# Issuing the first load ahead of the entry barrier in a row-wise relu-and-mean kernel

## The chip, the cores and the metric

The kernel runs on one core of a Trainium2 chip. The metric is device time in microseconds (us) per execution, taken as the median over several executions. "Span" is the length of one profiled execution, from its first to its last profiled instruction. The measured time of the same execution is 1.78 us longer than the span, in the kernel before (164.37 against 162.59).

Engine names in the profile: DVE is VectorE, ACT is ScalarE, POOL is GpSimd, SP is SyncE. A `q` behind a name (SPq) is the engine's sequencer: issues, semaphores, drains.

## The reference

```python
def setup_inputs():
    batch, seq, dim = 32, 512, 1024
    return {"x": np.random.randn(batch, seq, dim).astype(np.float32)}

def reference(x):
    relu_x = np.maximum(x, 0)
    return np.mean(relu_x, axis=-1).astype(np.float32)
```

The input is 64 MiB, the output 64 KiB. Each input value is used once.

## The kernel before

The input is seen as 128 partitions of 128 rows of 1,024 values. Seven loads bring 16 rows per partition each (8 MiB); the last 16 rows come in shrinking pieces, so that little work is left when the last byte lands. ACT and DVE take the rows in turn, each with one call that applies the relu and sums the row (in the profile, one long instruction and a short read of the sum).

```python
    in_pool = ctx.enter_context(tc.tile_pool(name="in", bufs=3))
    ...
    def rows(xt, lo, n, j0):
        for k in range(lo, lo + n):
            j = j0 + k
            (dve_row if j % 2 else act_row)(nc, xt[:, k, :], sums[:, j:j + 1])
    ...
    for t in range(full):                    # full = 7
        j0 = t * NB                          # NB = 16
        xt = in_pool.tile([P, NB, D], F32, name="xt")
        nc.sync.dma_start(out=xt, in_=xr[:, j0:j0 + NB, :])
        rows(xt, 0, NB, j0)
    ...
    for n in row_pieces:                     # 8, 4, 2, 1 rows
        nc.sync.dma_start(out=xt[:, lo:lo + n, :], in_=xr[:, j0 + lo:j0 + lo + n, :])
        lo += n
    for w in col_pieces:                     # the last row: 512, 256, 256 columns
        nc.sync.dma_start(out=last[:, c:c + w], in_=xlast[:, c:c + w])
        c += w
    ...                                      # the last rows, then the store of the result
```

With three buffers, the first three loads wait for nothing; each later one waits until its buffer has been read.

Ahead of all this stands an entry block that the kernel's author doesn't write. POOL sets four constants there, and then all five engines meet: PE, ACT, DVE and SP each run a drain, which adds one to a gather semaphore, and wait; POOL runs its own drain, waits for a count of four, and releases them. In the kernel before, SyncE's first load comes behind that wait.

Of the kernel before, what the change touches and what calls it, by code (L numbers as in the profile page):

```python
# [1 line left out]

# [4 lines left out]

F32 = mybir.dt.float32
ALU = mybir.AluOpType
ACT = mybir.ActivationFunctionType  # L10


def act_row(nc, src, acc):

    nc.scalar.activation(out=src, in_=src, func=ACT.Relu, accum_out=acc)  # L15


def dve_row(nc, src, acc, init=None):

    nc.vector.tensor_scalar(  # L20
        out=src, in0=src, scalar1=0.0, scalar2=init,
        op0=ALU.max, op1=ALU.add, accum_out=acc,
    )


@with_exitstack
def kernel(
    ctx: ExitStack,
    tc: tile.TileContext,
    x: bass.AP,  # L30
    out: bass.AP,
):
    nc = tc.nc
    P = nc.NUM_PARTITIONS
    xf = x.flatten_outer_dims()
    R, D = xf.shape
    assert R % P == 0
    J = R // P
    inv = 1.0 / D
    xr = xf.rearrange("(p j) d -> p j d", p=P, j=J)  # L40
    outr = out.flatten().rearrange("(p j) -> p j", p=P, j=J)
    xlast = xr[:, J - 1, :]

    NB = 16
    full = J // NB - 1

    row_pieces = [8, 4, 2, 1]
    assert sum(row_pieces) == NB - 1
    col_pieces = [512, 256, 256]
    assert sum(col_pieces) == D  # L50

    in_pool = ctx.enter_context(tc.tile_pool(name="in", bufs=3))
    res_pool = ctx.enter_context(tc.tile_pool(name="res", bufs=1))
    sums = res_pool.tile([P, J], F32)
    res = res_pool.tile([P, J], F32)
    part = res_pool.tile([P, 10], F32)
# [7 lines that stand above are left out]
    def finish(lo, hi):  # L64
        nc.gpsimd.tensor_scalar(  # L65
            out=res[:, lo:hi], in0=sums[:, lo:hi], scalar1=inv, scalar2=0.0, op0=ALU.mult, op1=ALU.add,
        )

    for t in range(full):
        j0 = t * NB  # L70
# [4 lines that stand above are left out]
    j0 = full * NB  # L75
    xt = in_pool.tile([P, NB, D], F32, name="xt")
    prev, last = xt[:, NB - 2, :], xt[:, NB - 1, :]
    lo = 0
    for n in row_pieces:
        nc.sync.dma_start(out=xt[:, lo:lo + n, :], in_=xr[:, j0 + lo:j0 + lo + n, :])  # L80
        lo += n
    c = 0
    for w in col_pieces:
        nc.sync.dma_start(out=last[:, c:c + w], in_=xlast[:, c:c + w])
        c += w

    finish(0, j0)
    lo = 0
    for n in row_pieces[:-1]:
        rows(xt, lo, n, j0)  # L90
        lo += n
    finish(j0, j0 + lo)



    act_row(nc, prev[:, :512], part[:, 0:1])
    dve_row(nc, prev[:, 512:], part[:, 1:2])
    nc.gpsimd.tensor_scalar(  # L98
        out=res[:, J - 2:J - 1], in0=part[:, 0:1], scalar1=part[:, 1:2], scalar2=inv, op0=ALU.add, op1=ALU.mult,
    )  # L100
    act_row(nc, last[:, :256], part[:, 2:3])
    dve_row(nc, last[:, 256:512], part[:, 3:4])
    nc.gpsimd.tensor_scalar(  # L103
        out=part[:, 4:5], in0=part[:, 2:3], scalar1=inv, scalar2=0.0, op0=ALU.mult, op1=ALU.add,
    )
    act_row(nc, last[:, 512:640], part[:, 5:6])
    dve_row(nc, last[:, 640:768], part[:, 6:7], init=part[:, 3:4])
    nc.scalar.activation(  # L108
        out=part[:, 7:8], in_=part[:, 5:6], func=ACT.Identity, scale=inv, bias=part[:, 4:5],
    )  # L110
    dve_row(nc, last[:, 768:], part[:, 8:9], init=part[:, 6:7])
    nc.vector.scalar_tensor_tensor(  # L112
        out=res[:, J - 1:J], in0=part[:, 8:9], scalar=inv, in1=part[:, 7:8], op0=ALU.mult, op1=ALU.add,
    )
    nc.sync.dma_start(out=outr, in_=res)


# [1 line left out]
_INS = ['x']  # L119
_OUTS = [((32, 512), 'float32')]  # L120


# [23 lines left out]
```

## Time and profile before

| | before |
|---|---|
| median time (3 runs, ahead of the prediction) | 164.64 us (164.58 to 164.67) |
| span of the profiled execution | 162.59 us |
| queue of the loads, share of 16 DMA engines' span | 96.2% |
| DVE busy, ACT busy | 46%, 43% |
| first load issued / first packet starts | 0.737 / 1.75 us |
| first compute | 22.94 us |
| last load landed on all 16 DMA engines | 159.11 us |

From the page of the kernel before (the fourth and fifth lines give the chain of work that ended last, the others busy time, mean time of one, and the idle time ahead of a group with what ended it):

```profile
span 162.6 us, 358 instructions
DVE 74.8 (46%) x135; ACT 69.6 (43%) x134; POOL 1.2 (1%) x8
q1 hardware_dynamic: 2160, 67.18, 96.2%
q14 instruction: 2, 0.02, 0.0%
DMA 84%; DVE 13%; SPq 1%; issue 0%; DVEq 0%
L20 DVE TENSOR_SCALAR_CACHE_REDUCE xt<-xt 128x1024 f32<-128x1024 f32 (+1 forms) x65 | 73.7, 1195 | 85.1 <-DMA xt<-in_x_dram 84.8
```

The loads' queue is full nearly from end to end, and DVE waits for loads more than it works. The packet records of the trace show how the stream moves: in its steady part, each DMA engine takes packets of 65,536 bytes in 2.42 us, one behind the other. The input is 64 such packets per engine, or 64 x 2.42 = 154.9 us. That rate is 27.1 GB/s per engine, and 16 x 27.1 = 434 GB/s agrees with the "fabric ceiling" of 435 GB/s in the Trainium skill, "DMA: Bandwidth & Descriptors", section "Specifications". So the time is a sum of three terms: what comes ahead of the stream, the stream, and what comes behind it. (The sum does not close exactly: the mean first packet starts at 2.21 us, and 2.21 + 154.9 = 157.1 us, while the last load lands at a mean of 158.45. Part of the 1.3 us between is that each engine's first packet takes 2.5 to 3.3 us instead of 2.42.)

The group of the entry block (line L130) in the kernel before: count, duration in ns (min/median/max), first and last start in us.

```profile
L130 SPq DRAIN  x1: 7/7/7, 0.0 to 0.0; - x1
L130 POOLq DRAIN  x1: 186/186/186, 0.3 to 0.3; - x1
L130 POOLq EVENT_SEMAPHORE  x2: 17/17/17, 0.5 to 0.6; - x2
L130 SPq EVENT_SEMAPHORE  x1: 17/17/17, 0.7 to 0.7; - x1
```

The timeline of the kernel before, the same stretch and the first compute: start, duration, engine, line, operation.

```profile
0.34 0.10 POOL L130 MEMSET const-uint8-127<- 128x1 uint8 x1
0.74 1.33 SPq L72 DMA_DIRECT2D xt<-in_x_dram  x3
22.94 1.06 ACT L15 ACTIVATE xt<-xt 128x1024 f32<-128x1024 f32 x1 [20.93 <-DMA xt<-in_x_dram]
```

SyncE arrives at 0.00 us and has nothing to do but wait; POOL's memsets and drain last until 0.49 us; SyncE is let go at 0.655 us and issues the first load at 0.737 us. (The third decimals are from the instruction records of the same trace.) That 0.74 us is the prize of the change.

The start of the chain that ended last, in the kernel before (start, duration, what):

```profile
0.74 0.38 SPq L72
1.11 0.05 issue
1.16 41.08 DMA xt<-in_x_dram
```

The chain follows the second load (issued at 1.16) back to its issue, and through it to the first issue and to the barrier.

### The profile page before, as it was taken

What the parts mean: (1) busy time and instruction counts of PE and PEld (TensorE: products, weight loads), DVE (VectorE), ACT (ScalarE), POOL (GpSimd) and SP (SyncE); (2) the same over time, 40 slices, a digit from 0 to 9 for tenths busy, and PEclk for the clock granted to TensorE, in tenths of its full rate; (3) what the DMA queues carried; (4) which work ended last, traced back from release to release, by engine and by line L of the source; (5) the groups of instructions that cost most, each with busy time, mean ns of one, the idle gap of its engine ahead of it and who ended that gap; (6) DMA issues with size and microseconds to landing.
All of it is one profiled execution on the core that took longest, in us unless ns stands there. A gap on an engine that the chain in (4) does not pass through costs nothing.

```text
span 162.6 us, 358 instructions
## 1 busy us (share of the span) xinstructions
DVE 74.8 (46%) x135; ACT 69.6 (43%) x134; POOL 1.2 (1%) x8
## 2 busy tenths in 40 slices
DVE  0000039900696008940099201990049800698993
ACT  3000039700694008920099002980049600696882
POOL 0000000000000000000000000000000000000001
DMA  7979989989988997997997998997998997998980
GB/s 258 516 322 451 516 355 419 516 371 403 516 387 387 516 435 339 516 435 339 516 484 326 484 484 355 451 500 339 451 500 355 435 516 306 451 435 379 415 334 17
DMA packets 2162, 67.19 MB, mean 413 GB/s; under 512 B 240, under 2 KB 624, under 8 KB 880
## 3 DMA queue, kind: packets, MB, share of 16 engines
q1 hardware_dynamic: 2160, 67.18, 96.2%
q14 instruction: 2, 0.02, 0.0%
HBM read 67.11 MB, written 0.07 MB: 413 GB/s over the span
## 4 chain that ended last, share of the span: by engine, by line
DMA 84%; DVE 13%; SPq 1%; issue 0%; DVEq 0%
DMA xt<-in_x_dram 84%; DVE xt L20 13%; SPq L80 1%; SPq L72 0%; DVE res L112 0%; DVEq L20 0%; DVEq L112 0%
## 5 line engine op out<-in xcount | busy, mean ns | idle before, releaser
L20 DVE TENSOR_SCALAR_CACHE_REDUCE xt<-xt 128x1024 f32<-128x1024 f32 (+1 forms) x65 | 73.7, 1195 | 85.1 <-DMA xt<-in_x_dram 84.8
L15 ACT ACTIVATE xt<-xt 128x1024 f32<-128x1024 f32 (+1 forms) x66 | 67.0, 1016 | 89.2 <-DMA xt<-in_x_dram 89.2
L15 ACT ACTIVATION_READ_ACCUMULATOR xt<-xt 128x1 f32 x66 | 12.3, 187 | 0.0
L20 DVE DVE_READ_ACCUMULATOR xt<-xt 128x1 f32 x65 | 5.4, 83 | 0.0
L65 POOL TENSOR_SCALAR res<-sums 128x112 f32<-128x112 f32 (+1 forms) x2 | 0.5, 252 | 157.2 <-DVE xt L20 157.2
L15 ACT ACT_TABLE_LOAD x1 | 1.3, 1283 | 0.7 <-PEq L130 0.7
L20 DVE TENSOR_SCALAR_CACHE_REDUCE xt<-xt,part 128x128 f32<-128x128 f32 (+1 forms) x2 | 0.8, 412 | 0.1
L108 ACT ACTIVATE part<-part 128x1 f32<-128x1 f32 x1 | 0.3, 294 | 0.1
L98 POOL TENSOR_SCALAR res<-part 128x1 f32<-128x1 f32 x1 | 0.3, 264 | 0.6 <-ACT xt L15 0.6
L112 DVE SCALAR_TENSOR_TENSOR res<-part 128x1 f32<-128x1 f32 x1 | 0.2, 159 | 0.1
L103 POOL TENSOR_SCALAR part<-part 128x1 f32<-128x1 f32 x1 | 0.2, 191 | 0.1
L20 DVE DVE_READ_ACCUMULATOR xt<-xt,part 128x1 f32 x2 | 0.2, 83 | 0.0
L130 POOL MEMSET const-bfloat16-1.0<- 128x1 bf16 x1 | 0.1, 101 | 0.0
L130 POOL MEMSET const-uint8-127<- 128x1 uint8 x1 | 0.1, 101 | 0.0
L130 POOL MEMSET const-float32-0.0<- 128x1 f32 x1 | 0.1, 98 | 0.2 <-issue 0.2
L130 POOL MEMSET const-float32-1.0<- 128x1 f32 x1 | 0.1, 98 | 0.0
## 6 DMA issues: line engine op xcount, KB each, us to landing
xt<-in_x_dram SPq DMA_DIRECT2D x1, 4096.0 KB, 39.0
xt<-in_x_dram SPq DMA_DIRECT2D x1, 2048.0 KB, 43.5
xt<-in_x_dram SPq DMA_DIRECT2D x1, 1024.0 KB, 45.5
xt<-in_x_dram SPq DMA_DIRECT2D x1, 512.0 KB, 46.4
xt<-in_x_dram SPq DMA_DIRECT2D x1, 256.0 KB, 46.5
xt<-in_x_dram SPq DMA_DIRECT2D x2, 128.0 KB, 42.7
xt<-in_x_dram SPq DMA_DIRECT2D x7, 49.0
out_dram<-res SPq DMA_DIRECT2D x1, 64.0 KB, 1.5
```

Source lines behind the costliest of these rows:

```text
L15: nc.scalar.activation(out=src, in_=src, func=ACT.Relu, accum_out=acc)
L20: nc.vector.tensor_scalar(out=src, in0=src, scalar1=0.0, scalar2=init, op0=ALU.max, op1=ALU.add, accum_out=acc,)
L65: nc.gpsimd.tensor_scalar(out=res[:, lo:hi], in0=sums[:, lo:hi], scalar1=inv, scalar2=0.0, op0=ALU.mult, op1=ALU.add,)
L80: nc.sync.dma_start(out=xt[:, lo:lo + n, :], in_=xr[:, j0 + lo:j0 + lo + n, :])
L98: nc.gpsimd.tensor_scalar(out=res[:, J - 2:J - 1], in0=part[:, 0:1], scalar1=part[:, 1:2], scalar2=inv, op0=ALU.add, op1=ALU.mult,)
L103: nc.gpsimd.tensor_scalar(out=part[:, 4:5], in0=part[:, 2:3], scalar1=inv, scalar2=0.0, op0=ALU.mult, op1=ALU.add,)
L108: nc.scalar.activation(out=part[:, 7:8], in_=part[:, 5:6], func=ACT.Identity, scale=inv, bias=part[:, 4:5],)
L112: nc.vector.scalar_tensor_tensor(out=res[:, J - 1:J], in0=part[:, 8:9], scalar=inv, in1=part[:, 7:8], op0=ALU.mult, op1=ALU.add,)
L130: nc = _bacc.Bacc("TRN2", target_bir_lowering=False, num_devices=1)
```

## The change

The intent: the first load waits for nothing and writes to a buffer that nobody uses at entry, so it needs no barrier in front. After the program is built, its instruction is taken out of the body and put into the entry block, ahead of SyncE's drain. Its readers stay behind the barrier and wait for the load's own semaphore.

```diff
+def issue_ahead_of_entry_barrier(nc):
+    entry, body = nc.cur_f.blocks[0].instructions, None
+    for block in nc.cur_f.blocks[1:]:
+        for k, ins in enumerate(block.instructions):
+            if ins.opcode == "DMACopy":
+                body, load = block.instructions, k
+                break
+        if body is not None:
+            break
+    first = body[load]
+    assert first.engine == mybir.EngineType.SP and not first.sync_info.on_wait
+    assert all(i.opcode == "DMACopy" or i.engine != first.engine for i in body[:load])
+    del body[load]
+    at = next(k for k, i in enumerate(entry) if i.engine == first.engine and i.opcode == "Drain")
+    entry.insert(at, first)
 ...
-    in_pool = ctx.enter_context(tc.tile_pool(name="in", bufs=3))
-    res_pool = ctx.enter_context(tc.tile_pool(name="res", bufs=1))
+    pools = ctx.enter_context(ExitStack())
+    in_pool = pools.enter_context(tc.tile_pool(name="in", bufs=3))
+    res_pool = pools.enter_context(tc.tile_pool(name="res", bufs=1))
 ...
     nc.sync.dma_start(out=outr, in_=res)
 
+    pools.close()
+    tc.close()
+    tc.compile()
+    issue_ahead_of_entry_barrier(nc)
```

The order of the executed instructions differs in this one place only, on SyncE, as the two traces show (358 instructions in both).

## The prediction

> **What bounds the kernel now.** The loads. In the page the hardware queue's packets take 96.2% of 16 engines' span, and the chain that ended last is 84% "DMA xt<-in_x_dram" and only 13% DVE. DVE is busy 46%, ACT 43%. The trace's packet records agree: each engine moves 65,536-byte packets of 2.42 us back to back; the 64 MiB input is 64 of them per engine, 64 x 2.42 = 154.9 us of a span of 162.6 us. Two or three loads are always queued, so the time is: start of the stream + about 155 us of stream + a tail.
>
> **The start, read from the timeline and the L130 and L72 groups.** SyncE's drain, its arrival at the entry barrier, stands at 0.00 us. POOL arrives last: four memsets from 0.24 us, its drain over at 0.49, its two semaphore instructions at 0.535 and 0.613. SyncE is let go at 0.655 and issues the first load from 0.737 to 1.114 us, the second from 1.164, the third from 1.639. The first packet starts at 1.75 us, 0.63 us after the issue ended (close to the "HWDGE first-byte" of about 600 ns in the Trainium skill, "DMA: Bandwidth & Descriptors", section "Latency and other measured facts").
>
> **What the change does.** It adds and removes no instruction; it moves one load issue (0.377 us) ahead of SyncE's drain. The load waits for nothing and its first readers stand behind the barrier. The issue should begin at about 0.00 instead of 0.737: 0.74 us saved, all on the critical path, since each later load follows the first through a full queue. First packet about 1.0 us instead of 1.75; first compute about 22.2 instead of 22.94; everything shifts by about 0.7 us to the end; the tail (last landing 159.11, end 162.59) keeps its length.
>
> **What it could cost.** SyncE now arrives at the barrier at about 0.40 us instead of 0.01. POOL's drain ends only at 0.49, so the barrier should still be released at about 0.65, by a margin of about 0.1 us. Even if late, it would hold only the second issue, needed some 20 us later.
>
> **Prediction.** 164.64 - 0.72 = 163.92 us (0.4% faster), 163.55 to 164.3 for 8 in 10. Faster by over 2% (3.3 us): 0.01; within 2%: 0.97; slower by over 2%: 0.02.
>
> **What would show it.** (1) The first SPq load at about 0.0 in the timeline, the second still at about 0.74. (2) The barrier's times unchanged. (3) The first compute near 22.2. (4) Gaps between later landings unchanged (19.35 us between the second and third loads), mean GB/s near 415, span near 161.9. (5) From the last landing to the end 3.5 us as before.
>
> **What would make it wrong.** (a) If SyncE's drain waits for the load's data and not just for its issue, the barrier would open only at about 22 us, the queue would run dry once for 1 to 2 us, and the kernel would be about 1 us slower. (b) If the profile's zero moves with the first issue, the span may show less or more than the measured time. (c) The staggered start of the 16 engines (first packets from 1.75 to 3.07 us, 3.0 us long instead of 2.42) may be shaped by the second issue's closeness; spread out, it could give another 0.2 to 0.5 us. (d) The instruction fetch at 87.2 us (two packets of 8,192 bytes, 0.31 us) delays two engines; where it falls may move the end by a few tenths.

## More of the kernel before

The line numbers of the profile shift (L130 is now L155, L72 is L92).

## The result, and the profile after

The changed kernel took 163.97 us (median of 4 runs, 163.88 to 164.14), beside 164.65 us (4 runs, 164.58 to 164.67) for the kernel before: 0.68 us less. The ratio is 0.9961, with a 95% interval of 0.9943 to 0.9978. Ratios here are the mean time of one kernel's fast runs over that of the other's of the same rounds, so not quite the ratio of the medians. A second measurement on another occasion (after_again, below) gave 163.89 beside 164.56 us, 0.67 us less and the same ratio.

From the page of the changed kernel:

```profile
span 162.1 us, 358 instructions
q1 hardware_dynamic: 2160, 67.18, 96.6%
DMA 84%; DVE 13%; SPq 1%; issue 0%; DVEq 0%
L20 DVE TENSOR_SCALAR_CACHE_REDUCE xt<-xt 128x1024 f32<-128x1024 f32 (+1 forms) x65 | 73.7, 1195 | 84.7 <-DMA xt<-in_x_dram 84.3
```

The group of the entry block (L155) in the changed kernel:

```profile
L155 POOLq DRAIN  x1: 186/186/186, 0.3 to 0.3; - x1
L155 POOLq EVENT_SEMAPHORE  x2: 17/17/17, 0.6 to 0.7; - x2
L155 SPq DRAIN  x1: 131/131/131, 0.4 to 0.4; - x1
L155 SPq EVENT_SEMAPHORE  x1: 17/17/17, 0.7 to 0.7; - x1
```

The timeline of the changed kernel:

```profile
0.00 2.07 SPq L92 DMA_DIRECT2D xt<-in_x_dram  x3
0.34 0.10 POOL L155 MEMSET const-uint8-127<- 128x1 uint8 x1
22.36 1.06 ACT L15 ACTIVATE xt<-xt 128x1024 f32<-128x1024 f32 x1 [20.30 <-DMA xt<-in_x_dram]
```

The first load is issued at 0.00 us. SyncE's drain, behind it, now lasts 131 ns instead of 7 and ends at 0.556 us, after POOL's at 0.485, so SyncE has become the last to arrive and the barrier opens 0.046 us later (0.701 instead of 0.655). The first compute begins 0.58 us earlier.

The start of the chain that ended last, in the changed kernel:

```profile
0.72 0.07 issue
0.78 40.87 DMA xt<-in_x_dram
```

Read as it stands, this says that the barrier still bounds the kernel, since the chain begins with the second load's issue at 0.78 us, straight behind the barrier. A look at the experiments shows that it doesn't: those 40.87 us are for the most part the second load's wait behind the first one's packets.

Where did the time come from? The trace records, for each load, when each of the 16 DMA engines raised the load's semaphore. Their mean and their last are told apart here, because they behave differently:

| us | before | after | gain |
|---|---|---|---|
| first load issued | 0.737 | 0.000 | 0.74 |
| first packet, mean of 16 engines (first to last) | 2.21 (1.75 to 3.07) | 1.44 (1.01 to 2.16) | 0.77 |
| first load landed, mean of 16 engines | 22.50 | 21.85 | 0.65 |
| fourth load landed, mean | 80.55 | 79.89 | 0.66 |
| last load landed, mean | 158.45 | 157.79 | 0.66 |
| last load landed, slowest engine | 159.11 | 158.62 | 0.49 |
| end of the span | 162.59 | 162.10 | 0.49 |

The shift arrives at the first load and stays, to the end, within 0.02 us of the engines' mean in this pair of traces. What lies behind the last landing is 3.48 us in both. Two things are odd. The mean landing gains 0.65 us of the 0.74. And in this pair of traces the slowest engine, which sets the end, gains only 0.49, though the medians of the timed runs differ by 0.68. The experiments take this up.

### The profile page after: what moved, and what is told of

Same layout as the page of the kernel before. It is cut to its first block, busy times and chain, and to the rows that moved or that the text cites. A ratio compares the mean times of both kernels' runs of the same rounds, so it can differ in the third digit from the quotient of the medians.

```text
span 162.1 us, 358 instructions
## 1 busy us (share of the span) xinstructions
DVE 74.7 (46%) x135; ACT 69.6 (43%) x134; POOL 1.2 (1%) x8
## 3 DMA queue, kind: packets, MB, share of 16 engines
q1 hardware_dynamic: 2160, 67.18, 96.6%
## 4 chain that ended last, share of the span: by engine, by line
DMA 84%; DVE 13%; SPq 1%; issue 0%; DVEq 0%
DMA xt<-in_x_dram 84%; DVE xt L20 13%; SPq L100 1%; DVE res L132 0%; DVEq L20 0%; DVEq L132 0%; SPq L92 0%
## 5 line engine op out<-in xcount | busy, mean ns | idle before, releaser
L155 POOL MEMSET const-bfloat16-1.0<- 128x1 bf16 x1 | 0.1, 101 | 0.0
L155 POOL MEMSET const-uint8-127<- 128x1 uint8 x1 | 0.1, 101 | 0.0
L155 POOL MEMSET const-float32-0.0<- 128x1 f32 x1 | 0.1, 98 | 0.2 <-issue 0.2
L155 POOL MEMSET const-float32-1.0<- 128x1 f32 x1 | 0.1, 98 | 0.0
```

The lines of the kernel that those rows point to most:

```text
L155: nc = _bacc.Bacc("TRN2", target_bir_lowering=False, num_devices=1)
```

## The experiments

The theory: only the issue of the first load is on the critical path; the barrier has some 20 us of slack behind it; every tenth by which the first issue moves is a tenth of the time. The rivals: (R1) the stream has slack, and only part of a shift reaches the end; (R2) the second issue counts as well, by how closely it follows the first; (R3) the lost 0.16 us of the slowest engine belongs to the earlier start and will always be lost.

Eight kernels ran. All gave correct results.

### after_again: the changed kernel once more

No edit.

> The changed kernel once more, for a second trace. In the first pair of traces the first load's issue moved by 0.74 us, the mean landing of the 16 engines by 0.65 us on every load, but the last landing and the span only by 0.49 us, because the spread between the engines' landings grew from 1.18 to 1.34 us after two instruction fetches (8,192 bytes each) at 84 to 87 us. Theory (the lost 0.16 us is chance: where the fetches fall): the time stays 0.6 to 0.75 us under the kernel before, and the spread after the fetches is another number, 1.1 to 1.4 us, with the mean landing again 0.65 us early. Rival (it is a property of the earlier start): the spread is again 1.34 us and the span again 162.1 us.

Measured: 163.89 us (163.79 to 164.04) beside 164.56; ratio 0.9961 (0.9949 to 0.9973). In its trace the first load landed at a mean of 21.76 us, the last at 157.87, on the slowest engine at 158.49; span 162.05. The spread of the fifth load's landings, after the fetches, was 1.32 us, and that of the last load 1.10 us, against 1.34 and 1.21 in the first trace of the same kernel and 1.18 and 1.09 in the kernel before.

What follows: taken alone, this trace doesn't decide between the theory and R3. Its spread (1.32 us) and its span (162.05 us) are near what R3 said (1.34 and 162.1), and the mean gained 0.74 us at the first load and 0.58 us at the last, not 0.65 throughout. R3 falls on other figures. The timed runs have spans too: 162.6 to 163.1 us, with a median of 162.8, in the 11 runs of the kernel before, and 162.0 to 162.3, with a median of 162.1, in the 5 runs here. So the end gains 0.7 us, and not 0.49. The trace of the kernel before was a lucky one: its run, 164.37 us, was faster than all the timed runs in that measurement (164.58 to 164.67). And the spread at the fifth load doesn't go with the early issue: it is 1.13 to 1.39 us in the traces of after, after_again, after_slow, three_ahead and between, and 1.18 and 1.29 us in before and before_slow. Two traces of the same kernel differ by 0.08 us in the last load's mean landing and by 0.13 us in its slowest one; the 0.67 to 0.68 us of the medians is the figure to believe.

### before_slow and after_slow: a longer barrier in both kernels

The edit, shortened (the helper that moves the memsets is left out):

```diff
+    scratch = res_pool.tile([P, 3, 1024], F32)
+    for k in range(3):
+        nc.gpsimd.memset(scratch[:, k, :], 0.0)
 ...
+    pool_work_ahead_of_drain(nc)     # moves the three memsets ahead of POOL's drain
```

In after_slow this stands beside the change; in before_slow the first load keeps its old place.

> The kernel before with the same three POOL memsets ahead of POOL's drain. Theory: every microsecond of barrier ahead of the first load is a microsecond of time, so the kernel is slower by the same D that the trace of after_slow shows (2 to 4 us, within 0.2 us of D). Rival (the stream of loads has slack that takes up part of a late start): slower by less than 0.7 D.

> The changed kernel with three extra POOL memsets (128x1024) ahead of POOL's drain, so that the entry barrier opens D us later (D is read from the trace, expected 2 to 4 us). Theory (only the first load's issue is on the path, the barrier has some 20 us of slack behind it): time as the changed kernel within 0.15 us, first compute still near 22.35 us, second load issued D later. Rival (the second load's issue counts too, by how closely it follows the first): the start stagger of the 16 engines shrinks from 1.15 us and the time falls by 0.2 to 0.5 us, or it rises by a part of D.

The timeline of before_slow:

```profile
0.37 2.73 POOL L97 MEMSET scratch<- 128x1024 f32 x3
3.41 1.32 SPq L113 DMA_DIRECT2D xt<-in_x_dram  x3
25.80 1.06 ACT L15 ACTIVATE xt<-xt 128x1024 f32<-128x1024 f32 x1 [21.12 <-DMA xt<-in_x_dram]
```

The timeline of after_slow, from two windows (the first line merges all three issues; the second shows that the second load is issued at 3.41 us, behind the barrier):

```profile
0.00 4.21 SPq L113 DMA_DIRECT2D xt<-in_x_dram  x3
3.41 0.81 SPq L113 DMA_DIRECT2D xt<-in_x_dram  x2
22.41 1.06 ACT L15 ACTIVATE xt<-xt 128x1024 f32<-128x1024 f32 x1 [17.72 <-DMA xt<-in_x_dram]
```

And the start of the chain that ended last, in after_slow:

```profile
3.34 0.07 issue
3.41 38.31 DMA xt<-in_x_dram
```

| | time, us | median less that of the same kernel without the memsets, us |
|---|---|---|
| before | 164.56 | |
| before_slow | 167.45 (167.21 to 167.56) | +2.89 |
| after_again | 163.89 | |
| after_slow | 164.05 (163.70 to 164.43) | +0.16, within the scatter |

The memsets moved the barrier by 2.67 us (SyncE let go at 3.327 instead of 0.655). In the kernel before, the first issue moved by the same 2.67 us and the time by 2.89; its mean landings moved by 2.76 (first load) and 2.85 us (last). In the changed kernel the second load's issue moved by 2.62 us and the time stayed. (before_slow also builds its program in the changed kernel's way, with the pools closed and the program compiled early, so that way of building is not what gains the time.)

What follows: the theory holds on both sides, to about 0.2 us. The kernel before lost 0.22 us more than the 2.67, a little over the 0.2 us allowed, and the changed kernel 0.16 instead of at most 0.15; both are as large as the scatter, and were not looked into. R1 falls: nothing of a late start is taken up later. The chain's start is shown to be misleading: in after_slow it begins at 3.34 us, behind a barrier that is 2.6 us later, and yet the span (161.9 us) is no longer than that of the changed kernel. The 2.6 us are simply missing in the wait that follows it (38.31 instead of 40.87 us). R2's hoped-for gain from a second issue that follows later is not there either: the first packets' starts spread over 0.92 us instead of 1.15, their mean came 0.05 us earlier than in after_again, and the time didn't fall.

### three_ahead: all three free loads ahead of the barrier

```diff
-    issue_ahead_of_entry_barrier(nc)
+    for _ in range(3):
+        issue_ahead_of_entry_barrier(nc)
```

> All three loads that wait for nothing are issued ahead of SyncE's drain. Theory: nothing more to gain, 163.97 us within 0.15 us, since the second and third loads are needed only some 20 and 40 us later; the barrier opens about 0.9 us later than in the changed kernel and this is not seen in the time. Rival (the closeness of the second issue shapes the start of the 16 engines): the starts of the first packets spread over more than 1.15 us and the time rises by 0.1 to 0.4 us.

Measured: 163.78 us (163.76 to 164.13); ratio to before 0.9958 (0.9946 to 0.9971), so not to be told from the changed kernel's 0.9961 (the median is 0.19 us under the 163.97 that the expectation named, 0.11 under after_again). The second load was issued at 0.426 us, straight behind the first; the barrier opened at 1.649 us. The first packets began at 1.00 to 2.06 us, with a mean of 1.43, as in the changed kernel (1.44, 1.42).

What follows: nothing more is to be had from the second and third loads, and the closeness of the second issue does not shape the start by more than the scatter: with the second issue at 0.43, 0.77 and 3.41 us, the first packets' mean is 1.43, 1.42 and 1.37 us and the time 163.78, 163.89 and 164.05 us. R2 falls from both sides.

### between: the load between SyncE's arrival and its wait

```diff
-    entry.insert(at, first)
+    entry.insert(at + 1, first)
```

> The first load is issued between SyncE's arrival at the barrier (its drain) and its wait, so the arrival is not held up by the issue. Theory (the barrier's own times are off the path): arrival at 0.00, issue from about 0.03 us, the barrier opens at 0.655 us as in the kernel before, and the time is that of the changed kernel, 163.9 us within 0.15 us. Rival (the later barrier of the changed kernel, 0.685 to 0.701 us, costs time): about 0.05 us faster than the changed kernel, which this number of runs could hardly tell.

The entry block (L155) in this kernel:

```profile
L155 SPq DRAIN  x1: 7/7/7, 0.0 to 0.0; - x1
L155 POOLq EVENT_SEMAPHORE  x2: 17/17/17, 0.5 to 0.6; - x2
```

Measured: 163.93 us (163.71 to 164.17); ratio 0.9961 (0.9949 to 0.9974). The drain is back at 7 ns and the barrier opens at 0.656 us, as in the kernel before; the first load is issued at 0.081 us (0.03 was expected).

What follows: the 131 ns of the drain come from the load in front of it, and they cost no time that these runs could show (0.05 us was at stake, which they could hardly tell). The drain does not wait for the load's data, which would have been some 22 us; it waits about a tenth of a microsecond more than with no load ahead.

### two_queues and quarters: two tries at a quicker start

The 16 DMA engines start one after the other, over about 1.1 us. If that were the making of the first load's row descriptors, two issuers or a smaller first load should shorten it. Edits, both on top of the change and shortened: other loads keep their form, and the helper's own edit for two_queues is left out. In two_queues both halves are moved ahead of their engine's drain; in quarters the first of the four is moved ahead of SyncE's drain.

```diff
two_queues:
+        if t == 0:
+            nc.sync.dma_start(out=xt[:, :NB // 2, :], in_=xr[:, :NB // 2, :])
+            nc.scalar.dma_start(out=xt[:, NB // 2:, :], in_=xr[:, NB // 2:NB, :])
quarters:
+        if t == 0:
+            for r in range(4):
+                nc.sync.dma_start(out=xt[r::4], in_=xr[r::4, :NB, :])
```

> The first load in two halves of 8 rows, one issued by SyncE and one by ScalarE, both ahead of their drains. Theory (the start of the stream is set by the first issue and the 16 engines' rate): no gain, 163.9 us within 0.2 us. Rival (the engines' start stagger of 0.9 to 1.2 us is the time in which one issuer's descriptors are made, and two issuers halve it): the starts of the first packets spread over about 0.6 us, the mean start falls by 0.2 to 0.4 us and the time with it.

> The first load in four loads of 32 partitions each (every fourth partition), the first of them ahead of SyncE's drain. Fewer rows in the first load. Rival of two_queues' kind (the stagger is the making of 128 row descriptors): the 16 engines start within about 0.3 us, mean start about 0.35 us earlier, time up to 0.35 us shorter. Theory (the start is already as good as it gets, and each of the small loads has a cost): 163.9 us to 164.5 us.

Measured: two_queues 163.86 us (163.81 to 164.00), ratio 0.9958 (0.9946 to 0.9970), the same as the change alone; the first load landed at a mean of 21.86 us on one queue and 22.04 on the other. The first packets of SyncE's half began at 0.99 to 2.68 us, with a mean of 1.50 (1.44 in the changed kernel), and those of ScalarE's half behind them, at 2.83 to 3.90: two issuers did not shorten the stagger. quarters 164.27 us (164.03 to 164.72), ratio 0.9983 (0.9969 to 0.9997): about 0.3 us slower than the changed kernel, though the two intervals just overlap. Its first issue took 0.543 us though it is a quarter of the size (0.377 us for the whole load), the first packet began at 1.32 us, and the starts still spread over 0.98 us.

What follows: neither is a way to gain. In quarters the longer issue explains 0.17 us of the later first packet (0.543 - 0.377), and 1.32 - 1.01 = 0.31 us is seen; the rest is open (the first packet came 0.78 us after the end of the issue instead of 0.63), as is what sets the stagger.

### more_fetches: what the instruction fetches cost

The two packets of the queue named "instruction" in the page are instruction fetches of 8,192 bytes. In the kernel before they ran at 87.19 and 87.22 us; the loads' packets that followed them took 2.89 and 3.03 us instead of 2.42, and the spread of the 16 engines' landings grew from 0.78 us (fourth load) to 1.18 (fifth). Since they move the engine that sets the end, their cost was tested by making more of them: 448 one-column memsets on DVE. In the program as built, 443 of them stand ahead of DVE's first row, so they run while it waits for the first load.

```diff
+    scratch = res_pool.tile([P, full, 64], F32)
 ...
         rows(xt, 0, NB, j0)
+        for k in range(64):
+            nc.vector.memset(scratch[:, t, k:k + 1], 0.0)
```

> The changed kernel with 448 tiny memsets more on DVE, in the time in which it waits for the first load. An instruction fetch is a packet of 8,192 bytes, so 128 instructions of 64 bytes; 448 more instructions are 3 to 4 more fetches. Theory (each fetch holds one of the 16 engines up by about 0.3 to 0.6 us, and the last engine sets the end): 5 to 6 fetch packets in the span, mean landing of the last load within 0.15 us of the changed kernel's 157.8 to 157.9 plus 0.1, the spread of landings 1.3 to 2.2 us, the time 0.2 to 0.8 us longer than 163.9. Rival (fetches are lost in the noise): time within 0.1 us of 163.9 and spread at most 1.3 us.

The queues in the page of more_fetches, and the time from issue to landing (min/median/max) of its 8 MiB loads:

```profile
q1 hardware_dynamic: 2160, 67.18, 94.5%
q14 instruction: 6, 0.05, 0.1%
DMA to landing us min/median/max: 25.6/48.7/63.1
```

The last line has its counterpart in the changed kernel:

```profile
DMA to landing us min/median/max: 22.3/49.1/59.8
```

The timeline of more_fetches, DVE's memsets (the bracket gives the idle time ahead) and the first compute:

```profile
2.99 3.64 DVE L96 MEMSET scratch<- 128x1 f32 x128 [0.38 <-issue]
8.61 3.63 DVE L96 MEMSET scratch<- 128x1 f32 x128 [1.97 <-issue]
14.42 3.58 DVE L96 MEMSET scratch<- 128x1 f32 x126 [2.19 <-issue]
25.65 1.22 DVE L20 TENSOR_SCALAR_CACHE_REDUCE xt<-xt 128x1024 f32<-128x1024 f32 x1 [7.65 <-DMA xt<-in_x_dram]
```

Measured: 167.46 us (167.45 to 167.53), 3.5 us more than the changed kernel and far outside what the theory expected (0.2 to 0.8 us). The page shows 6 fetches instead of 2; by the packet records they ran at 6.85, 12.51, 18.33, 24.13, 89.17 and 155.79 us. Fifteen engines landed the first load by 22.41 us, much as in the changed kernel (22.34); the sixteenth landed it at 25.62. The packet records show why: each of the first four fetches starts as one packet of that engine ends, two packets after the fetch before it, and the load packet (65,536 bytes) behind each takes 2.95, 3.08, 3.08 and 3.07 us instead of 2.42. With the fetches' own 0.31 to 0.33 us that is 0.84 to 0.99 us for each, 3.8 us in all, of which 3.2 us show beyond the slowest of the other fifteen. The fifth fetch, at 89.17 us, didn't touch that engine's lag; the last, at 155.79 us, added 1.0 to it. A load has landed only when its slowest engine is done, so the end moved with it: last landing 162.26 instead of 158.6 us. The memsets themselves are out of the question as the cause: all but five were over at 18.0 us, DVE then waited 7.65 us for the load, and the last five took 0.09 us at 34.80.

What follows: the theory had the direction and missed the size, because it let the fetches fall on several of the 16 engines, and took 0.3 to 0.6 us for each. DVE's fetches fell on one engine: at the first four ACT had run 3 instructions, so they are DVE's. DVE's pauses come after 63 instructions and then every 128, and at the last fetch it had run 574 (63 + 4 x 128 = 575), so that one is its own as well. At 89.17 us, where the lag stayed, ACT had run 63, so that one is likely ACT's. The two fetches of the kernel before hit two engines, since the packets behind them overlap (2.89 us from 87.50 us, 3.03 us from 87.53). With the fetch's own 0.31 us they cost 0.78 and 0.92 us; those of the changed kernel cost 0.60 and 0.94 in the first trace. This is a likely reason why the slowest engine, and with it the end of one execution, scatters by a few tenths more than the mean of the 16, but it was not shown: that ACT's fetches keep to a second engine was not tested, and a kernel with no fetch in its stream was not built.

No experiment points to a version that beats the changed kernel: three_ahead, two_queues and between are within its scatter.

## Why the prediction was right

The time was predicted at 163.92 us and measured at 163.97, within the range. Point by point:

1. *What bounds the kernel: the stream of loads.* Right. The queue's share went from 96.2% to 96.6%, the chain remained 84% loads, and 2.67 us of late start cost 2.89 us (before_slow).
2. *The first issue moves from 0.737 to about 0.00 us.* Right: 0.000. The first packet came at 1.01 us (predicted 1.0), again 0.63 us after the end of the issue, close to the "HWDGE first-byte" of about 600 ns in the Trainium skill, "DMA: Bandwidth & Descriptors", section "Latency and other measured facts" (which does not say from when it counts).
3. *All 0.74 us on the critical path, about 0.72 to be seen.* Right in kind; the measured 0.67 to 0.68 us is 0.04 to 0.05 smaller than the sum, which lies inside the scatter. The mean landing of the first load gained 0.65 us in one trace and 0.74 in the other.
4. *The barrier's times unchanged, SyncE at the barrier at about 0.40 us, second issue still at about 0.74.* Wrong by a little, without effect. The drain behind the load takes 131 ns instead of 7, SyncE arrives at 0.54 to 0.56 us, and the barrier opens 0.03 to 0.05 us later. The fallback in the prediction, that a late barrier would only hold the second issue, is what after_slow shows.
5. *First compute near 22.2 us.* Measured 22.36 and 22.26.
6. *Gaps between landings (19.35 us), about 415 GB/s, span near 161.9, tail 3.5 us.* 19.35 us, 415 GB/s, 162.1 and 162.05, 3.48 us (3.56 in the second trace). The span is a little over the forecast because that was counted from the lucky trace of the kernel before.
7. *The named dangers.* (a) The drain doesn't wait for the data. (b) The profile's zero did not move in a way that matters: DVE's drain stands at 0.129 us before and 0.125 after, and time minus span is 1.78 us in both. (c) The second issue's closeness does not shape the start beyond the scatter (after_slow, three_ahead). (d) The instruction fetches do move the end by tenths, and by more than their 0.31 us: 0.6 to 1.0 us for the one engine they fall on.

## What to carry to other kernels

In a kernel that streams loads from end to end, the moment of the first load's issue is worth its full difference (here 0.74 us earlier gave 0.68 us, and 2.67 us later cost 2.89), while the barrier and the second load behind it have slack (2.6 us of it was shown here, and the first load's 20 us suggest more); so put the one load that waits for nothing in front of whatever the start waits for, and expect no more than the time that it waited. When a chain of waits begins at a later load's issue, ask whether that load is queued behind another one's packets: if it is, the wait shrinks as the issue comes later, and the chain's start bounds nothing. For a few tenths of a microsecond, compare medians of several runs and means over the DMA engines, since two traces of one kernel differ by as much (0.13 us in the slowest engine here, and 0.08 to 0.09 us even in the means).

## What the Trainium skill lacked or had wrong

- "Runtime: NRT & Kernel Launch", section "Instruction fetch mechanics", says that the instruction memory is refilled in 16 KiB blocks of 256 instructions and that the cost of crossing a boundary is "mostly hidden". Here fetches were of 8,192 bytes, and DVE's memsets paused every 128 instructions; each fetch beside a full stream of loads held one DMA engine up by 0.6 to 1.0 us, and DVE itself stood for 0.4, 2.0 and 2.2 us at three such boundaries.
- The same page does not say on which DMA engines one compute engine's fetches fall. In more_fetches four of DVE's in a row fell on the same one, and the kernel became 3.5 us slower, since every load waits for its slowest engine.
- No page looked up gives the time of a drain behind a load's issue: 7 ns with no load ahead, 125 to 131 ns behind whole loads on SyncE, 367 ns behind the strided quarter load. It does not wait for the data.
- "DMA: Bandwidth & Descriptors" has no time for the issue itself as a function of the load's form: 0.33 to 0.45 us for most loads here, 0.54 us for the first load of every fourth partition, and 0.91 us for the third load of the changed kernel. Its section "Specifications" gives about 27 GiB/s per engine; the steady packets here show 27.1 GB/s (65,536 bytes in 2.42 us), which is 25.2 GiB/s.
